# Cross attention in a decoder trunk: the queries of two heads as seven block products, laid between halves of keys and values

## The chip, the cores and the metric

The kernel runs on one core of one Trainium2 chip. The metric is the device time of one execution in microseconds (us). All data are float32; the matrix products are made by TensorE from two parts of each operand.

## The reference, cut to what matters

A trunk of two layers over 512 tokens of 1024 columns. Each layer runs a feed-forward network (FFN), a token mixer (layer 0: differential attention, layer 1: a pooling mixer), the cross attention into 256 memory tokens, and a second FFN, each followed by a layer norm. The change is in the cross attention:

```python
def memory_cross_attention(x, mem, wq, wkv, wo):      # x (1, 512, 1024), mem (1, 256, 1024)
    q = (x @ wq).reshape(B, S, 4, 256)                # 4 heads of 256 columns
    k, v = jnp.split(mem @ wkv, 2, axis=-1)
    ...
    s = jnp.einsum('bshd,bmhd->bhsm', q, k) * 256 ** -0.5
    p = jax.nn.softmax(s, axis=-1)
    o = jnp.einsum('bhsm,bmhd->bshd', p, v).reshape(B, S, 1024)
    return o @ wo
...
x = layer_norm(a * x + memory_cross_attention(x, mem, ...), ln_g[i, 2], ln_b[i, 2])
```

## The kernel before

**Numbers in two parts.** An operand is split into a rounded high part (a copy on ScalarE, names ending in h: `wh`, `xh`) and a low part (a subtraction on VectorE, `wl`, `xl`); `split` does this (lines 120 and 121), `split_scaled` with a factor (124 to 126). A product is three matmuls, high x high, high x low, low x high: `mm3`, lines 205 to 207. So nearly all matmuls of the profile stand on these three lines, and are told apart by their tiles.

**Tokens and weights.** The tokens lie as X0 to X3 (128 tokens each). After a layer norm a token tile is transposed on TensorE (line 489, tile `pt`) and split into `xh` and `xl`, one tile for each half of the columns. Raw weights are fetched by SyncE's queue (`raw_cols`, line 233: 8 x 128 rows by 256 columns, 1 MB, tiles of 8 KB a partition) into two buffers `raw`, then split into `wh` and `wl` (five buffers of each in the stages outside the FFN).

**The cross attention.** Queries of a head are two column tiles of 128, each 8 k x 3 matmuls over 512 tokens into the tiles `xq`, then scaled and split into `q`. Keys of a head (`xa_k`) are two tiles of 8 x 3 matmuls over 256 memory tokens into `pk`; values (`xa_v`) two of 8 x 3 into `pv`. A head's attention (`xa_head`) makes scores `xs`, the softmax into `p`, transposes `pt`, and `xo`, split into `oT`. `xa_main` walks the four heads: keys and values, then queries. `weave` runs `xa_main` and lets `xa_side` (the heads' attention) advance one step each time the main work's estimated nanoseconds have grown by a gap of 2500; a head's side work starts 3000 after its queries are ready. The output projection (`to_tokens`, tiles `ps`) runs in two halves of four k, the second with the residual sum and the layer norm.

In layer 0 the memory is fetched (`load_memory`, line 1314, tiles `p`) while the attention before is still at its output projection, and transposed (line 1327) into `mem0` to `mem7`. In layer 1 the memory, the keys and values of heads 0 and 1 and the keys of head 2 are made between the pooling mixer's work (`early_kv`). There, a list `late` holds work of the last token tile, which `turn_late` runs between matmuls, so the first head's queries are made in two halves of 256 tokens. Two of the first weights of a stage are held back by `split_weights` until a given point of the layer norm (`GATES`).

**The FFN's form of a product.** The FFN already makes some products of two blocks by two blocks with seven products instead of eight (`second_factors` and `up`): with the tokens as halves of tokens by halves of columns, six further factors are formed from sums, of which tiles `xe` hold the split parts; the weights' sums are made by DMAs that add to what is in the tile (`accum_op`, issued on GpSimd's queue, line 666), between two uses of the same tile.

Of the kernel before, what the change touches and what calls it, by code (L numbers as in the profile page):

```python
# [17 lines left out]
P = 128  # L18
# [26 lines left out]
GATES = {"xa": (1, 2)}  # L45

# [63 lines left out]
class Trunk:  # L110
    def __init__(self, tc, a, out, upto=8):
        self.tc, self.nc, self.a, self.out, self.upto = tc, tc.nc, a, out, upto
        self.side, self.late, self.gates = [], [], []
        self.ln_next_gb, self.kv_bufs = None, 8
# [95 lines left out]
    def weave(self, main, side, gap, lead=0):  # L210
# [3 lines left out]
        for ns in main:  # L214
            self.clock += ns
# [44 lines left out]

    def raw_heads(self, w, c0):
# [30 lines left out]
    def rows(self, w, k0, kn, c0, homes=None):  # L292


        got = []
        for k in range(0, kn, 4):
            n = min(4, kn - k)
            raw = self.raw_tile((4, S))
            r0 = (k0 + k) * P
            self.nc.sync.dma_start(  # L300
                raw[:, :n], w[r0 : r0 + n * P, c0 : c0 + S].rearrange("(k p) n -> p k n", p=P)
            )
            if homes:
                got += [home() for home in homes]
                for j, t in enumerate(got):
# [151 lines left out]
    def turn(self, t, half, tag="px"):  # L457
# [6 lines left out]
        if self.ln_next == "ffn":  # L464
# [544 lines left out]
    def da_values(self, h, vs):  # L1009

        raw = self.raw_cols(self.a["da_w_qkv"][0], 2 * D + h * P)
        ws = self.wide(raw)
# [232 lines left out]
    def pool_mixer(self, layer, ln):  # L1245
# [37 lines left out]
        wg = self.wide(self.pool_w)  # L1283
        self.begin_ln(layer, ln, 1.0)
        for t in range(NT):
# [16 lines left out]
            self.turn_late()  # L1302
# [33 lines left out]
    def xa_kv(self, w, h):  # L1336
        kt = self.keys.pop(0) if self.keys else (yield from self.xa_k(w, h))
        return kt, (yield from self.xa_v(w, h))

    def xa_k(self, w, h, raw=None, then=None, turn=True):  # L1340
        rk = raw or self.raw_cols(w, h * 256)
        ps = self.mm("pk").rearrange("p (c n) -> p c n", c=2)
        for j in range(2):
            with self.after(self.x_split if raw and not then else ()):
                wk = self.cols(rk, j)
            if then and j == 1:
                then()
            for k in range(KC):
                yield self.mm3(
                    ps[:, j], (wk[0][:, k], wk[1][:, k]), self.memT[k], k == 0, k == KC - 1  # L1350
                )
        kt = self.kv_tiles((P, 2, MEM))
        if turn:
            self.turn_late()
# [8 lines left out]
    def xa_v(self, w, h, raw=None):  # L1363
        wv = self.wide(raw or self.raw_cols(w, D + h * 256))
# [10 lines left out]
    def xa_head(self, qs, kt, v):  # L1375
# [34 lines left out]
        for c in range(2):  # L1410
# [4 lines left out]
            o = self.pair("oT")  # L1415
            self.split(o[0], o[1], po)
            self.oT.append(o)
            yield

    def early_kv(self, layer, ln, heads, raws):  # L1420
        w, keys = self.a["xa_wkv"][layer], {}

        def load_more():
            keys[1] = self.raw_cols(w, 256)
# [7 lines left out]
        self.keys.append((yield from self.xa_k(w, heads, turn=False)))  # L1432
# [191 lines left out]
```

## Time and profile before

| | us |
|---|---|
| runs | 1934.05, 1938.31, 1939.21 (median 1938.31) |
| profiled execution | 1932.35 |
| its span in the trace | 1930.6 |
| PE busy | 1902.1 (99%) |
| DVE, ACT, POOL busy | 1566.3, 1022.2, 315.0 (81%, 53%, 16%) |
| mean granted clock of TensorE | 0.998 |

In the rows of the profile, PE is TensorE's matmuls, PEld its weight loads, DVE is VectorE, ACT ScalarE, POOL GpSimd and SP SyncE; "q" behind a name is the engine's queue. A row of a timeline gives the start, the time, the engine, the line, the operation, out<-in, the shape and, in brackets, the idle time ahead of it with what ended it. A matmul's duration overlaps the next one's: the interval between two starts is what it costs in a stream. A row of a window gives the stretch, its length, busy time and count of PE, PEld, DVE, ACT and POOL, the granted clock, the share of the DMA engines and GB/s. A row of DMA issues ends with KB each and the median us from issue to landing.

### The profile page before, as it was taken

To read this page: it belongs to the slowest core of one execution; us is meant where nothing else is said; L and a number is where in the kernel's file an instruction comes from. 1 tells how busy PE (TensorE), PEld (TensorE's weight loads), DVE (VectorE), ACT (ScalarE), POOL (GpSimd) and SP (SyncE) were. 2 spreads that over 40 slices of the span, in tenths; PEclk is the share of its full clock that TensorE was granted. 3 is DMA by queue.
4 is the path that set the end of the run, shared out by engine and by line. 5 is a ranking of instruction groups with operands and counts; after the bars stand their busy time and mean duration, and the time that the engine had idled before them with its cause. 6 is when DMAs were issued, how large, how long until landed. Compare 5 with 4: busy or idle time off the path is not lost.

```text
span 1930.6 us, 32520 instructions
## 1 busy us (share of the span) xinstructions
PE 1902.1 (99%) x13114; PEld 1740.5 (90%) x13114; DVE 1566.3 (81%) x2200; ACT 1022.2 (53%) x1580; POOL 315.0 (16%) x276
## 2 busy tenths in 40 slices
PE   8999999999999999999999999999999999999998
PEld 8999998888778888999998999999889889999997
DVE  7888889888867557888888988898887568988886
ACT  6555454567655435655554655455445436555553
POOL 2112121111210001211210321112040012111210
PEclk9999999999999999999999999999999999999999
DMA  9978772322134316977686587778244356867861
GB/s 239 220 169 182 175 138 77 90 80 74 48 117 142 110 66 186 186 175 164 139 194 179 104 179 168 177 162 185 89 153 134 115 140 120 181 158 170 183 133 56
DMA packets 246743, 277.96 MB, mean 144 GB/s; under 512 B 8256, under 2 KB 212544, under 8 KB 246592
## 3 DMA queue, kind: packets, MB, share of 16 engines
q0 software_dynamic: 92928, 92.29, 31.1%
q1 hardware_dynamic: 153664, 183.59, 29.2%
q8 instruction: 103, 1.69, 0.3%
q14 instruction: 48, 0.39, 0.1%
HBM read 273.75 MB, written 2.10 MB: 143 GB/s over the span
## 4 chain that ended last, share of the span: by engine, by line
PE 80%; DVE 12%; ACT 3%; DMA 2%; issue 2%; POOL 1%; SPq 1%; DVEq 0%; ACTq 0%; POOLq 0%
PE x L205 7%; PE x L206 7%; PE x L207 7%; PE z L206 4%; PE z L205 4%; PE z L207 4%; PE ps L205 4%; PE ps L207 4%; PE ps L206 4%; PE px L205 2%; PE px L207 2%; PE px L206 2%; DVE wl L121 2%; PE y L207 2%; PE x L681 2%
## 5 line engine op out<-in xcount | busy, mean ns | idle before, releaser
L666 POOL DMA_DIRECT2D ra<-in_ffn_w_in_dram x132 | 170.3, 1309 | 993.5 <-DVE wl L121 815.2
L120 ACT CAST wh<-ra 128x1024 fp32r<-128x1024 f32 x184 | 193.7, 1053 | 218.9 <-PE x L206 67.5
L121 DVE TENSOR_TENSOR wl<-ra,wh 128x1024 fp32r<-128x1024 f32 x184 | 223.8, 1220 | 73.0 <-ACT wh L120 72.5
L120 ACT CAST wh<-rc 128x1024 fp32r<-128x1024 f32 x136 | 143.1, 1053 | 118.6 <-PE x L206 43.1
L205 PE MATMUL x<-xe,wh 128*128 128x256 f32 x704 | 195.0, 277 | 0.0
L206 PE MATMUL x<-xe,wh 128*128 128x256 f32 x704 | 194.8, 277 | 0.0
L207 PE MATMUL x<-xe,wl 128*128 128x256 f32 x704 | 194.8, 277 | 0.0
L121 DVE TENSOR_TENSOR wl<-rc,wh 128x1024 fp32r<-128x1024 f32 x136 | 164.6, 1219 | 28.4 <-ACT wh L120 28.1
L120 ACT CAST wh<-b 128x1024 fp32r<-128x1024 f32 x112 | 117.8, 1052 | 131.3 <-PE x L206 67.7
L121 DVE TENSOR_TENSOR wl<-b,wh 128x1024 fp32r<-128x1024 f32 x112 | 136.7, 1220 | 40.2 <-ACT wh L120 40.2
L205 PE MATMUL x<-xh,wh 128*128 128x256 f32 x544 | 151.1, 278 | 0.0
L206 PE MATMUL x<-xl,wh 128*128 128x256 f32 x544 | 150.6, 277 | 0.0
L207 PE MATMUL x<-xh,wl 128*128 128x256 f32 x544 | 150.6, 277 | 0.0
L206 PEld LDWEIGHTS x<-xe,wh 128*128 128x128 f32 x704 | 132.5, 188 | 1.4
L205 PEld LDWEIGHTS x<-xe,wh 128*128 128x128 f32 x704 | 132.1, 188 | 1.3
L207 PEld LDWEIGHTS x<-xe,wl 128*128 128x128 f32 x704 | 132.2, 188 | 0.0
L121 DVE TENSOR_TENSOR wl<-raw,wh 128x1024 fp32r<-128x1024 f32 x64 | 81.8, 1285 | 38.8 <-ACT wh L120 38.2
L206 PEld LDWEIGHTS x<-xl,wh 128*128 128x128 f32 x544 | 102.5, 188 | 0.7
L205 PEld LDWEIGHTS x<-xh,wh 128*128 128x128 f32 x544 | 102.1, 188 | 0.7
L207 PEld LDWEIGHTS x<-xh,wl 128*128 128x128 f32 x544 | 102.1, 188 | 0.0
L207 PE MATMUL y<-xh,wl 128*128 128x256 f32 x352 | 98.4, 280 | 1.2
L206 PE MATMUL z<-xl,wh 128*128 128x256 f32 x352 | 97.5, 277 | 0.7 <-DVE xl L121 0.7
(429 smaller groups left out, 6291.6 us busy)
## 6 DMA issues: line engine op xcount, KB each, us to landing
ra<-in_ffn_w_in_dram POOLq DMA_DIRECT2D x132, 512.0 KB, 6.7
rc<-in_ffn_w_in_dram SPq DMA_DIRECT2D x88, 512.0 KB, 5.8
b<-in_ffn_w_out_dram SPq DMA_DIRECT2D x76, 512.0 KB, 4.8
ra<-in_ffn_w_in_dram SPq DMA_DIRECT2D x44, 512.0 KB, 5.4
rc<-in_ffn_w_in_dram POOLq DMA_DIRECT2D x44, 512.0 KB, 6.7
raw<-in_xa_wkv_dram SPq DMA_DIRECT2D x16, 1024.0 KB, 5.4
raw<-in_da_w_qkv_dram SPq DMA_DIRECT2D x16, 512.0 KB, 5.2
raw<-in_xa_wq_dram SPq DMA_DIRECT2D x8, 1024.0 KB, 4.9
```

Of the source, the lines that this page charges most:

```text
L120: self.nc.scalar.copy(hi, src),
L121: self.nc.vector.tensor_sub(lo, src, hi.bitcast(F32)),
L205: mm(out, w[0], x[0], start=start, stop=False, skip_group_check=again)
L206: mm(out, w[0], x[1], start=False, stop=False, skip_group_check=again)
L207: self.last_mm = mm(out, w[1], x[0], start=False, stop=stop, skip_group_check=again)
L666: nc.gpsimd.dma_start(t, source(*block), accum_op=ALU.add)
L681: self.last_mm = nc.tensor.matmul(ps[:, j], v[i][:, k, j * P : (j + 1) * P], x[l][:, k], start=n == i == l == 0, stop=n == 7 and i == 1, s ...
```

## The change

For each layer, the queries of heads 0 and 1, and of heads 2 and 3, are now one product of two blocks by two blocks each (`xa_queries`: 512 tokens as two halves, 1024 columns as two halves of k, two heads as two column blocks), made by seven products of 24 matmuls over 256 tokens. Factors 0 and 1 are the tokens 0 and 1 as they were; the other factors come from `xa_factors`, which transposes tokens 2 and 3, forms the sums and splits them, in four steps. The weights' sums come from accumulating DMAs on GpSimd's queue. `XA_ORDER` lays the parts out by hand for each layer: a digit is the next part (half of keys, half of values) of that head, "q" and "r" the next product of the first and second pair, "s" the next step of the factors, "Q" and "R" the point from which a pair's two heads are open to the side work; a head's attention so can start only when its whole pair is done.

Around it, raw weights lie in tiles of 4 KB (half of a head's keys or values, 512 KB, or two k of the output's weights), five of them in layer 0, four in layer 1; the stage's `wh` and `wl` have four buffers, not five; `pT`, `oT` and `q` have fewer or wider buffers, and later `oT` tiles and the layer norm's gains use the six factor tiles `xe`. The weave's gap is 2100. The diff, without small helpers:

```diff
+XA_ORDER = ("0000s00ss" "qq1q11qq1q11qQ" "r222r2r22rr3rrR33333", "qsqs2qsq2sq3qqQ" "r2r3rr33rrrR33")
...
+    def raw_quarter(self, w, r0, c0, width):
+        raw = self.raw_tile((4 * 256 // width, width))
+        rows = w[r0 : r0 + P * 4 * 256 // width, c0 : c0 + width]
+        self.last_load = self.nc.sync.dma_start(raw, rows.rearrange("(k p) n -> p k n", p=P))
+        return raw
+    def raw_keys(self, w, h):
+        return [self.raw_quarter(w, 0, h * 256 + j * P, P) for j in range(2)]
+    def raw_values(self, w, h):
+        return [self.raw_quarter(w, r, D + h * 256, 256) for r in (0, S)]
...
-        for j in range(0, 8, 4):
+        for half in raw:
             t = self.hl([P, 4, 256])
-            self.split_weights(t[0], t[1], raw[:, j : j + 4])
+            self.split_weights(t[0], t[1], half)
...
+        got, n = [], self.raw_rows
+        for k in range(0, kn, n):
+            raw = self.raw_tile((n, S))
             r0 = (k0 + k) * P
...
-        if self.ln_next == "ffn":
+        if self.ln_next != "da":
...
-    def xa_kv(self, w, h):
-        kt = self.keys.pop(0) if self.keys else (yield from self.xa_k(w, h))
-        return kt, (yield from self.xa_v(w, h))
-
-    def xa_k(self, w, h, raw=None, then=None, turn=True):
-        rk = raw or self.raw_cols(w, h * 256)
+    def xa_kv(self, w, h, turn=None):
+        kt = self.keys.pop(0) if self.keys else None
+        if not kt:
+            kt = yield from self.xa_k(w, h, turn=turn)
+            yield None
+        self.kv.append((kt, (yield from self.xa_v(w, h))))
+    def xa_k(self, w, h, raw=None, then=None, turn=None):
+        rk = raw or self.raw_keys(w, h)
         ps = self.mm("pk").rearrange("p (c n) -> p c n", c=2)
         for j in range(2):
+            wk = self.hl([P, KC, P])
             with self.after(self.x_split if raw and not then else ()):
-                wk = self.cols(rk, j)
+                self.split_weights(wk[0], wk[1], rk[j])
             if then and j == 1:
                 then()
             for k in range(KC):
                 yield self.mm3(
                     ps[:, j], (wk[0][:, k], wk[1][:, k]), self.memT[k], k == 0, k == KC - 1
                 )
+            yield None
...
-            o = self.pair("oT")
-            self.split(o[0], o[1], po)
-            self.oT.append(o)
+            if c == 0:
+                o = self.pair("oT" if len(self.oT) < 4 else "xe", (P, 2, S))
+            self.split(o[0][:, c], o[1][:, c], po)
+            self.oT.append((o[0][:, c], o[1][:, c]))
...
+    def xa_factors(self):
+        nc, F, H = self.nc, self.factors, 2 * P
+        a11, a12, a21, s1 = (self.tmp("oT", (P, 4, H)) for i in range(4))
+        def part(i, x, o=slice(0, H)):
+            self.split(F[i][0][:, :, o], F[i][1][:, :, o], x)
+        for t in (2, 3):
+            o = slice(t % 2 * P, (t % 2 + 1) * P)
+            pts = []
+            for half in range(2):
+                pt = self.aux("pt", ("py", "yz")[half]).rearrange("p (c n) -> p c n", c=4)
+                c0 = half * S
+                with self.behind():
+                    self.transpose4(pt, [self.X[t][:, c0 + j * P : c0 + (j + 1) * P] for j in range(4)])
+                pts.append(pt)
+            nc.scalar.copy(a21[:, :, o], pts[0])
+            nc.vector.tensor_tensor(s1[:, :, o], pts[1], a21[:, :, o], ALU.subtract)
+            part(3, s1[:, :, o], o)
+            part(2, pts[1], o)
+            yield
+        for r, (hi, lo) in zip((a11, a12), F):
+            nc.vector.tensor_tensor(r, hi.bitcast(F32), lo.bitcast(F32), ALU.add)
+        s2, s4, s3 = s1, a12, a21
+        nc.vector.scalar_tensor_tensor(s2, s1, -1.0, a11, ALU.mult, ALU.subtract)
+        nc.vector.scalar_tensor_tensor(s4, s2, -1.0, a12, ALU.mult, ALU.subtract)
+        part(6, s4)
+        yield
+        part(4, s2)
+        nc.vector.tensor_tensor(s3, a11, a21, ALU.subtract)
+        part(5, s3)
+        yield
+    def xa_queries(self, w, h, q):
+        nc, H = self.nc, 2 * P
+        def source(row, col):
+            c0 = (h + col - 1) * H
+            return w[(row - 1) * S : row * S, c0 : c0 + H].rearrange("(k p) n -> p k n", p=P)
+        def load(*block):
+            t = self.raw_tile((4, H))
+            nc.sync.dma_start(t, source(*block))
+            return t
+        def more(t, *block):
+            nc.gpsimd.dma_start(t, source(*block), accum_op=ALU.add)
+        def operand(raw):
+            v = self.hl([P, 4, H])
+            self.split_weights(v[0], v[1], raw)
+            return v
+        def product(ps, v, a, start=False):
+            x = self.factors[a]
+            for j in range(2):
+                o = slice(j * P, (j + 1) * P)
+                for k in range(4):
+                    yield self.mm3(
+                        ps[:, j], (v[0][:, k, o], v[1][:, k, o]), (x[0][:, k], x[1][:, k]),
+                        start and j == k == 0, j == 1 and k == 3, True,
+                    )
+        bank = lambda t: t.rearrange("p (j n) -> p j n", j=2)
+        halves = slice(0, H), slice(H, S)
+        scale = (D // XA_H) ** -0.5
+        def done(i, half, src, by):
+            hi, lo = (t[:, :, halves[half]] for t in q[i])
+            self.split_scaled(hi, lo, src, by)
+        ra = load(1, 1)
+        x = bank(self.aux("x", "px"))
+        v = operand(ra)
+        more(ra, 1, 2)
+        rc = load(2, 1)
+        yield from product(x, v, 0, True)
+        p1 = self.tmp("p", (P, 2, H))
+        nc.scalar.copy(p1, x)
+        yield None
+        y = bank(self.aux("y", "yz"))
+        v = operand(rc)
+        rd = load(2, 2)
+        yield from product(y, v, 1, True)
+        nc.vector.tensor_tensor(p1, y, p1, ALU.add)
+        q[0] = self.pair("q", (P, 2, S))
+        done(0, 0, p1, scale)
+        yield None
+        z = bank(self.aux("z", "yz"))
+        v = operand(ra)
+        more(ra, 2, 2)
+        yield from product(z, v, 3, True)
+        p5 = self.tmp("p", (P, 2, H))
+        nc.scalar.copy(p5, z)
+        yield None
+        v = operand(rd)
+        more(rd, 1, 2)
+        yield from product(z, v, 6)
+        yield None
+        v = operand(ra)
+        more(ra, 2, 1)
+        yield from product(x, v, 4)
+        u2 = self.tmp("p", (P, 2, H))
+        q[1] = self.pair("q", (P, 2, S))
+        nc.scalar.copy(u2, x)
+        nc.vector.tensor_tensor(u2, z, u2, ALU.add)
+        done(1, 0, u2, -scale)
+        yield None
+        yield from product(x, operand(rd), 5)
+        nc.vector.tensor_tensor(p5, x, p5, ALU.add)
+        done(1, 1, p5, -scale)
+        yield None
+        yield from product(x, operand(ra), 2)
+        done(0, 1, x, scale)
+        yield None
+    def part(self, units):
+        for ns in units:
+            if ns is None:
+                return
+            yield ns
     def xa_main(self, layer):
         wq, wkv = self.a["xa_wq"][layer], self.a["xa_wkv"][layer]
-        early = len(self.kv)
-        for h in range(XA_H):
-            if h >= len(self.kv):
-                self.kv.append((yield from self.xa_kv(wkv, h)))
-            kt, v = self.kv[h]
-            raw = self.raw_cols(wq, h * 256)
-            qs = []
-            ws = [self.cols(raw, c) for c in range(2)]
-            ps = [self.mm("xq") for c in range(2)]
-            for p in ((0, 2 * P), (2 * P, S)) if self.late else ((0, S),):
-                for c in range(2):
-                    yield from self.project(ps[c], ws[c], (p,))
-                    self.turn_late(max(len(self.late) - 1, 0) if c == 0 else 0)
-            for c in range(2):
-                q = self.pair("q")
-                self.split_scaled(q[0], q[1], ps[c], (D // XA_H) ** -0.5)
-                qs.append(q)
-            self.heads.append((self.clock, (qs, kt, v)))
-            if 0 < early and h + early < XA_H:
-                self.kv.append((yield from self.xa_kv(wkv, h + early)))
+        self.late, second = [], self.xa_factors()
+        qs = [[None] * 2 for n in range(2)]
+        works = {n: self.xa_queries(wq, 2 * i, qs[i]) for i, n in enumerate("qr")}
+        works.update((str(h), self.xa_kv(wkv, h)) for h in range(1, XA_H))
+        works["0"] = self.xa_kv(wkv, 0, lambda: next(second))
+        for n in XA_ORDER[layer]:
+            if n == "s":
+                next(second)
+            elif n in "QR":
+                i = "QR".index(n)
+                for j in range(2):
+                    q = [(qs[i][j][0][:, c], qs[i][j][1][:, c]) for c in range(2)]
+                    self.heads.append((self.clock, 2 * i + j, q))
+            else:
+                yield from self.part(works[n])
...
-            while h >= len(self.heads) or self.clock < self.heads[h][0] + 3000:
+            while h >= min(len(self.heads), len(self.kv)) or self.clock < self.heads[h][0] + 3000:
                 yield WAIT
-            yield from self.xa_head(*self.heads[h][1])
...
-        bufs = dict(q=8, oT=10, gb=2)
+        bufs = dict(xe=6, q=4, oT=4)
+        self.raw_rows = 2
         if layer == 0:
             self.kv, self.keys = [], []
             mem = self.side_pool("mem")
-            with self.other_pools():
+            with self.stage_pools(4, dict(raw=5), ("wh", "wl", "raw")):
                 self.stage["mem"] = mem
-                with self.phase_pool(("gb", "gb"), "p", pT=6, p=4, kv=8, _x=0, **bufs):
+                with self.phase_pool(("xe", "xe"), "p", pT=4, p=4, kv=8, _x=0, **bufs):
                     self.kvp = self.phase["kv"]
                     with self.tc.high_priority():
                         self.load_memory("p")
                     self.xa(layer, ln)
             self.close_side()
         else:
-            with self.later, self.phase_pool(("gb", "gb"), "p", _x=0, pT=6, p=4, **bufs):
+            with self.later, self.phase_pool(("xe", "xe"), "p", _x=0, pT=4, p=4, **bufs):
                 self.xa(layer, ln)
     def xa(self, layer, ln):
-        self.heads, self.oT = [], []
-        self.weave(self.xa_main(layer), self.xa_side(), 2500)
+        self.heads, self.oT, self.factors = [], [], self.factor_tiles()
+        self.weave(self.xa_main(layer), self.xa_side(), 2100)
         self.begin_ln(layer, ln, 1.0)
         kv = lambda: self.kv_tiles((P, S))
-        homes = [[lambda: self.pair("q")] * 4, [kv] * 4]
+        wide = [self.pair("q", (P, 2, S)) for k in range(2)]
+        views = [tuple(t[:, i] for t in pair) for pair in wide for i in range(2)]
+        homes = [[lambda v=v: v for v in views], [kv] * 4]
...
-            self.later.enter_context(self.other_pools(("wh", "wl", "mem", "raw")))
+            self.later.enter_context(self.stage_pools(4, dict(raw=4), ("wh", "wl", "mem", "raw")))
...
-                raws = [self.raw_cols(w, c) for c in (0, D)]
+                raws = [self.raw_keys(w, 0), self.raw_values(w, 0)]
...
```

More of the change, by code (lines that the diff above doesn't have):

```diff
@@ L214, in weave @@
         for ns in main:
+            ns = ns or 0
             self.clock += ns
@@ L1431, in early_kv @@
             self.kv.append((kt, (yield from self.xa_v(w, h, raws[1] if h == 0 else None))))
-        self.keys.append((yield from self.xa_k(w, heads, turn=False)))
+        self.keys.append((yield from self.xa_k(w, heads)))
+    def xa_factors(self):
[28 more added lines that the diff above has]
+        yield
```

27 lines of the change are left out of this document (13 added, 14 removed).

## The prediction, before the result

> **What bounds the kernel now.** I read the page first: busy shares, granted clock, chain.
>
> ```profile
> span 1930.6 us, 32520 instructions
> PE 1902.1 (99%) x13114; PEld 1740.5 (90%) x13114; DVE 1566.3 (81%) x2200; ACT 1022.2 (53%) x1580; POOL 315.0 (16%) x276
> PEclk9999999999999999999999999999999999999999
> PE 80%; DVE 12%; ACT 3%; DMA 2%; issue 2%; POOL 1%; SPq 1%; DVEq 0%; ACTq 0%; POOLq 0%
> ```
>
> TensorE is busy 99% of the span at a granted clock that never leaves the top tenth, and it carries 80% of the chain that ended last. Then I asked for the windows of the changed stage: layer 0's first head, the rest of its heads, and the heads of layer 1.
>
> ```profile
> 605.00:630.00 25.00, 25.00 (x172) 22.82 (x171) 14.88 (x21) 11.14 (x20) 0.00 (x0) 1.00 0.54 168
> 630.00:702.00 72.00, 72.00 (x447) 63.68 (x445) 38.40 (x60) 31.58 (x61) 0.00 (x0) 1.00 0.36 118
> 1492.00:1544.00 52.00, 52.00 (x306) 45.26 (x305) 27.32 (x47) 22.23 (x47) 0.00 (x0) 1.00 0.31 106
> ```
>
> In all three PE (first figure after the length) has no idle time, and VectorE (third pair) has 40 to 47% to spare. Two things follow. Every matmul taken out here shortens the run by its full time, and every new wait of PE costs its full time, since nothing of before's waits is there to be paid with it.
>
> **What is removed.** The price of a matmul is the interval between starts, since the durations overlap.
>
> ```profile
> L205 PE MATMUL xq<-xh,wh 128*128 128x512 f32 x112 | 45.1, 403 | 0.0
> L205 PE MATMUL x<-xe,wh 128*128 128x256 f32 x704 | 195.0, 277 | 0.0
> 605.04 0.40 PE L205 MATMUL xq<-xh,wh 128*128 128x512 f32 x1
> 616.24 0.28 PE L205 MATMUL pk<-mem0h,wh 128*128 128x256 f32 x1
> 618.97 0.28 PE L205 MATMUL pk<-mem0h,wh 128*128 128x256 f32 x1
> ```
>
> From 605.04 to 616.24 stand the 48 matmuls of head 0's queries (two column tiles, eight k, three products): 11.20 us, 0.2333 each. From 616.24 to 618.97 stand 24 of half the columns: 2.73 us, 0.1138 each. Before, the queries take 7 heads x 48 = 336 at 512 columns (112 on each of three lines, as the first row counts) and 96 at 256 for the eighth head, whose tokens are taken by halves: 336 x 0.2333 + 96 x 0.1138 = 78.4 + 10.9 = 89.3 us. After: seven products x 24 x four pairs of heads = 672 at 256 columns, 76.5 us. **Gain 12.8 us**; all other matmuls are the same in number. If the new ones run at 0.118 the gain is 10.0; if the eighth head's 96, which transposes interrupt, were worth 0.12, 13.4.
>
> **What is added beside PE.** Per layer VectorE gets six factors' sums and low parts and some more low halves of weights; by the count of instructions about 22 us more a layer, and ScalarE about 14. The same kinds of operation stand in the FFN's entry, back to back:
>
> ```profile
> 1605.20 1.28 DVE L380 SCALAR_TENSOR_TENSOR X<-X,rstd,gb 128x1024 f32<-128x1024 f32 x1
> 1606.40 0.68 DVE L631 TENSOR_TENSOR hb<-pt,hb 128x512 f32<-128x512 f32 x1
> 1607.00 1.21 DVE L611 TENSOR_TENSOR hb<-xh,xl 128x1024 f32<-128x1024 f32 x1
> 1608.14 0.68 DVE L121 TENSOR_TENSOR xl<-hb,xh 128x512 fp32r<-128x512 f32 x1
> ...
> 1622.01 1.22 DVE L121 TENSOR_TENSOR xe<-sr,xe 128x1024 fp32r<-128x1024 f32 x1
> 1623.14 1.22 DVE L644 TENSOR_TENSOR hb<-hb 128x1024 f32<-128x1024 f32 x1
> ```
>
> By intervals a scaled sum of 1024 columns costs 1.20 us, a plain one or a low half 1.13 to 1.14, one of 512 0.60. Over the whole stage the addition is hidden: 605 to 702 has 53.3 us of VectorE in 97, so about 75 in 90 afterwards. What matters is where it is needed at once. There are three such places.
>
> **Place 1: entry of layer 0.** The built program shows something the diff only implies. With the raw tiles at 4 KB and the extra factor tiles, the memory's raw tiles (p) now lie over tiles of the attention before: the first of the four loads waits for the last ps<-low matmuls and stands in SP's queue behind weight loads, the others wait for ScalarE's square of token 3 (rt). Before, they were issued 30 us earlier.
>
> ```profile
> 559.25 2.69 SPq L1314 DMA_DIRECT2D p<-in_mem_dram  x4
> 588.73 0.39 PE L207 MATMUL ps<-p,oT 128*128 128x512 f32 x1
> 590.64 0.88 PE L1327 MATMUL pt<-ident,p 128*128 128x128 f32 x6 [0.16 <-DVE xl L121]
> 591.27 0.36 PE L205 MATMUL pk<-mem0h,wh 128*128 128x256 f32 x1
> 590.51 0.67 DVE L357 SCALAR_TENSOR_TENSOR X<-X,ps 128x512 f32<-128x512 f32 x1
> 593.40 1.15 ACT L374 ACTIVATE rt<-X,mean 128x1024 bf16<-128x1024 f32 x1 [0.99 <-DVE mean L366]
> p<-in_mem_dram SPq DMA_DIRECT2D x4, 256.0 KB, 3.1
> ```
>
> Before, keys start at 591.27. After, token 3's sum ends about 590.5 on VectorE (no memory low halves stand ahead of it), one weight low half (1.13) and the mean follow, the square runs from about 591.9 to 593.1. Four issues took 2.69 us before; the first is released earlier here, so I put the last at about 594.0. It lands 3.1 later at 597.1, and its transposes (six took 0.88, four about 0.6) and their cast bring the keys to about 597.9. PE has nothing to fill this: in its order the 16 transposes and the 48 matmuls of keys stand right behind the last ps. **Loss 6.6 us**, 5 if the square comes a microsecond sooner and loads overlap better, 8 if the loads share the engines with the weight loads ahead of them.
>
> **Place 2: first pair of layer 0.** The weights' sums are made by accumulating DMAs on POOL's queue. After the third product (z) has split its weights, its tile takes one more block for the fifth product. Between the two PE has the 24 matmuls of z and about 12 others (2 of keys, 8 of scores, 2 of the fourth product): 36 x 0.114 = 4.1 us. The rest of the keys and the fourth product, which could hide the wait, stand behind the fifth product's first matmuls on PE.
>
> ```profile
> ra<-in_ffn_w_in_dram POOLq DMA_DIRECT2D x132, 512.0 KB, 6.7
> ra<-in_ffn_w_in_dram POOLq DMA_DIRECT2D x3, 512.0 KB, 5.9
> ra<-in_ffn_w_in_dram POOLq DMA_DIRECT2D x3, 512.0 KB, 9.6
> L120 ACT CAST wh<-ra 128x1024 fp32r<-128x1024 f32 x184 | 193.7, 1053 | 218.9 <-PE x L206 67.5
> ```
>
> The first row is the median of the run, the others are those of 764 to 782 us (quiet SP queue) and of 735 to 760 (DMA share 0.81). The stage has a share of 0.54, nearer to the quiet case: 6.2 + 1.05 for the cast = 7.3 against 4.1. **Loss 3.2 us** (2.5 to 4.5 from 5.9 and the median, more in a rival). The Trainium skill, "DMA: Bandwidth & Descriptors", section "Anatomy of one DMA — SWDGE (gpsimd) path", fits such a transfer by 2.0 us plus its bytes at 436 GB/s: for 512 KB an estimate of 3.2 us, and the sum would be 3.2 us lower. The trace's 5.9 to 9.6 us for an accumulating one disagree, and the measurement decides.
>
> **Place 3: first pair of layer 1.** Here no keys or values of head 0 are left to cover the factors. VectorE's order from token 3's mean to the low part of the factor that the fourth product needs holds 7 weight low halves (7.9 us), 4 plain sums or low parts of 1024 (4.6), 4 scaled ones (4.8) and 9 of 512 columns (5.4): 22.7 us.
>
> ```profile
> 1461.74 1.28 DVE L380 SCALAR_TENSOR_TENSOR X<-X,rstd,gb 128x1024 f32<-128x1024 f32 x1 [0.32 <-POOL rstd L376]
> 1462.95 1.22 DVE L247 TENSOR_TENSOR wl<-raw,wh 128x1024 fp32r<-128x1024 f32 x1
> 1467.90 1.06 PE L489 MATMUL pt<-ident,X 128*128 128x128 f32 x8 [0.47 <-DVE X L380]
> 1464.55 0.28 PE L205 MATMUL xq<-xh,wh 128*128 128x256 f32 x1
> ```
>
> Before, the instruction at this point starts at 1462.95; after, one more weight low half (1.13) stands ahead of it and I allow 0.4 for the mixer's fourth weight buffer, so about 1464.5, and the factor is ready at 1487.2. PE meanwhile has from 1464.55 (delayed by about 1) three products, head 2's values and 2 of keys, 122 x 0.1138 = 13.9 us, and 16 transposes (2 x 1.06): done at 1481.6. **Stall 5.6 us**, 4 to 7. Before's 0.47 there is not saved, it becomes part of it.
>
> **The rest.** The last xo stands inside the next projection's group: about +0.5 us. The second pairs have 9 us or more of PE work between each accumulating load and its use, so nothing (up to 2). Plain loads halve in size and double in number on SP's queue; the DMA share of 0.36 to 0.54 hides them. The pooling mixer has four weight buffers instead of five: nothing, +-1.
>
> **Sum** on the profiled execution: 1932.35 (span 1930.6) - 12.8 + 6.6 + 3.2 + 5.6 + 0.5 = 1935.45, **+3.1 us**. The median of the runs is 1938.31, so 1941.4. With all ends together: -13.4 + 5 + 2.5 + 4 + 0 - 1 = -2.9 to -10 + 8 + 4.5 + 7 + 0.5 + 3 = +13; as these don't all fall one way, 1935 to 1949 for this case.
>
> **Rivals.**
> A. *The gain comes through.* Places 1 and 3 cost little: the memory loads go out as the attention's tiles come free, earlier than I chained them, and the factors of layer 1 keep ahead of PE. For it: VectorE's spare share of the windows, and the same construction in the FFN's entry, where VectorE runs the whole chain between 1605 and 1623. Against it: the waits stand in the program, and PE's order has nothing to slide in. With 1 us left at each: -12.8 + 1 + 1 + 3.2 + 0.5 = about -7, so 1931. Chance 0.24.
> B. *Accumulating loads are slow in the whole stage* (slower). They share the engines with SP's weight loads, as in the 9.6 us row. Then place 2 costs 9.6 + 1.05 - 4.1 = 6.6, and in the second pairs, where 9 us of cover stand against 10.7, three steps a layer lose 1.7: 10 us in all. Sum 3.1 + 3.4 + 10 = +16.5, so 1955; it decides from about 8 us a load on. Half of that is likelier: 1949. Chance 0.17.
> C. *Halving the columns does not halve a matmul* (slower). Each one carries a weight load of 188 ns, and if that set the pace at 256 columns, 672 x 0.188 = 126 us would replace 89, +37 us. Against it: 0.1138 us between starts in row upon row. Chance 0.04. The Trainium skill, "TensorE: Matmul & The Clock Gate", section "Back-to-back issue gap", gives a sustained spacing of about 81 ns at 128 columns and 131 at 512; between them an estimate of 98 at 256 makes the queries 53 us before and 66 after, so a loss of 13 in place of the gain. The trace shows 113.8 and 233.3, in proportion, and decides.
>
> **How the numbers follow.** The forecast's case has 0.55. A measurement of this kernel tells about 0.3%, 5.8 us, from no change: of that case 0.35 lies within it, 0.19 above +5.8, 0.01 below -5.8. Faster: 0.25. Same: 0.35. Slower: 0.19 + 0.17 + 0.04 = 0.40. The range takes in A's value and the lower half of B: 1929 to 1951.
>
> **What would show it.** In the profile after: 672 matmuls at 256 columns about 0.114 apart and no xq at 512; the memory loads issued after 590 with PE idle about 6 us before the first pk of layer 0; an idle time of about 3 us ahead of the fifth product's x<-xe near 620, ended by the cast of an accumulated tile; and one of about 5 us near 1482, ended by VectorE's low part of xe. It is wrong if PE stays busy through these three places, or if idle time shows ahead of the second pairs or in the mixer of layer 1.

## The result: slower by 1%, and the profile after

| | before | after |
|---|---|---|
| median of the runs, us | 1936.37 (4 runs) | 1955.26 (4 runs, 1953.64 to 1957.92) |
| profiled execution / span, us | 1932.35 / 1930.6 | 1954.08 / 1952.1 |
| ratio to before, 95% interval | | 1.0099 [1.0085, 1.0113] |

The forecast was 1941.4 in 1929 to 1951; the measured time is 18.9 us over before's and outside the range. The page of the changed kernel, first the rows that answer to those of before:

```profile
span 1952.1 us, 33221 instructions
PE 1903.1 (97%) x13354; PEld 1754.3 (90%) x13354; DVE 1606.5 (82%) x2244; ACT 1048.0 (54%) x1614; POOL 336.8 (17%) x292
PEclk9999999999998999999999999999999999999999
PE 73%; DVE 15%; DMA 4%; ACT 4%; issue 2%; POOL 1%; SPq 1%; DVEq 0%; ACTq 0%; POOLq 0%
```

Two differences of these rows hold the whole loss. The span less PE's busy time, its idle time, went from 1930.6 - 1902.1 = 28.5 to 49.0 us: 20.5 us more. And PE's busy time rose by 1.0 us where 12.8 less were counted. VectorE got 40 us and ScalarE 26 more, where 44 and 28 were counted. In the chain PE lost 7 points of its share; DVE and DMA took five of them, ACT one.

PE's longest waits (what waited, for what, us in total, times, longest), before and after; the waits for X's load are the kernel's start:

```profile
PE pt L489 <- DMA X<-in_x_dram: 7.1, 2, 4.1
PE ps L206 <- DVE wl L121: 3.1, 1, 3.1
PE sc L1070 <- DVE a L121: 1.7, 2, 1.3
```

```profile
PE pt L1345 <- DMA p<-in_mem_dram: 9.2, 3, 7.7
PE pt L506 <- DMA X<-in_x_dram: 6.4, 2, 4.2
PE pt L506 <- DVE xl L124: 3.8, 1, 3.8
PE ps L209 <- DVE wl L124: 2.9, 1, 2.9
PE x L208 <- ACT wh L123: 2.5, 1, 2.5
```

The three foreseen places are there, with their times in the timelines:

```profile
592.18 2.22 SPq L1332 DMA_DIRECT2D p<-in_mem_dram  x4
...
596.04 0.66 PE L1345 MATMUL pt<-ident,p 128*128 128x128 f32 x2 [7.68 <-DMA p<-in_mem_dram]
...
601.37 0.56 PE L208 MATMUL pk<-mem0h,wh 128*128 128x256 f32 x1
...
630.97 0.58 PE L208 MATMUL x<-xe,wh 128*128 128x256 f32 x1 [2.53 <-ACT wh L123]
...
1487.01 1.04 ACT L123 CAST wh<-raw 128x1024 fp32r<-128x1024 f32 x1 [4.18 <-DMA raw<-in_xa_wkv_dram]
...
1490.66 1.08 PE L506 MATMUL pt<-ident,X 128*128 128x128 f32 x4 [3.82 <-DVE xl L124]
...
1498.46 2.20 ACT L123 CAST wh<-raw 128x1024 fp32r<-128x1024 f32 x2 [3.88 <-DMA raw<-in_xa_wq_dram]
...
1500.71 0.38 PE L208 MATMUL pk<-mem0h,wh 128*128 128x256 f32 x1 [0.95 <-ACT wh L123]
...
1502.14 0.38 PE L208 MATMUL z<-xe,wh 128*128 128x256 f32 x1 [0.93 <-ACT xe L123]
```

```profile
p<-in_mem_dram SPq DMA_DIRECT2D x4, 256.0 KB, 5.1
```

The memory's loads go out at 592.18, as worked out, PE idles 7.7 us for the first of them, they take 5.1 us to land in the median, and the keys start at 601.37. The fifth product's first matmul waits 2.5 us for the cast of an accumulated tile. In layer 1 PE waits 3.8 us, not for the factors' sums but for token 3's low half, whose VectorE queue stood behind a weight cast on ScalarE that a late load held up for 4.2 us. Waits near the factors come later, four between 1500 and 1504 (0.95, 0.93, 0.56 and 0.31 us); the first is for weights that ScalarE cast only after waiting 3.9 us for an accumulating load.

What the prediction had no term for is in the windows (length, busy time and count of PE, PEld, DVE, ACT, POOL, then the granted clock):

```profile
586.00:604.00 18.00, 8.80 (x43) 7.28 (x42) 13.17 (x18) 7.57 (x13) 2.49 (x2) 0.72 0.59 175
592.83:603.07 10.24, 5.52 (x24) 4.75 (x25) 6.34 (x8) 2.80 (x7) 1.08 (x1) 0.50 0.87 256
...
630.38:637.19 6.81, 6.22 (x29) 6.22 (x30) 2.36 (x2) 1.92 (x3) 2.43 (x2) 0.50 0.98 216
632.00:638.00 6.00, 6.00 (x33) 6.00 (x33) 1.48 (x3) 1.24 (x2) 1.29 (x1) 0.57 1.06 198
...
638.00:704.00 66.00, 63.26 (x520) 61.51 (x519) 41.93 (x62) 34.30 (x61) 5.12 (x4) 1.00 0.61 150
...
1490.54:1493.93 3.39, 3.27 (x16) 3.30 (x17) 3.39 (x5) 1.88 (x3) 1.32 (x1) 0.50 0.50 149
1504.19:1507.59 3.40, 3.40 (x18) 3.40 (x17) 1.80 (x2) 1.82 (x2) 0.11 (x1) 0.50 1.13 170
```

With each of these groups of waits the granted clock falls. From 632 to 638 PE is busy all the time and gets 33 matmuls done, where 6 us hold 52 at 0.1138. The starts there stand 0.21 us apart:

```profile
632.21 0.41 PE L208 MATMUL pk<-mem0h,wh 128*128 128x256 f32 x1
632.42 0.41 PE L209 MATMUL pk<-mem0l,wh 128*128 128x256 f32 x1
```

So a wait of 2.5 us is followed by 6.2 us at half pace (630.97 to 637.2): 29 matmuls, which at 0.1138 take 3.3 us, so 2.9 are lost. In the four stretches that the clock spends at 0.50, PE works 5.52 + 6.22 + 3.27 + 3.40 = 18.4 us; in the same proportion about 8.6 us of that are lost, well over half of the 13.8 by which PE's busy time is over the count. (A fifth stretch, in the mixer, has its like in the trace of before.) Another 1.7 us lie in the matmuls: the 672 new ones take 82.1 us from start to start, or to their own end where PE then waits, of which 2.2 are the half clock's, and before's 432 took 91.0 by the same measure. That is a gain of 11.1 and not 12.8. The other 3.5 I could not place.

### The profile page after: what moved, and what is told of

Same layout as the page of the kernel before. It is cut to its first block, busy times and chain, and to the rows that moved or that the text cites. A ratio compares the mean times of both kernels' runs of the same rounds, so it can differ in the third digit from the quotient of the medians.

```text
span 1952.1 us, 33221 instructions
## 1 busy us (share of the span) xinstructions
PE 1903.1 (97%) x13354; PEld 1754.3 (90%) x13354; DVE 1606.5 (82%) x2244; ACT 1048.0 (54%) x1614; POOL 336.8 (17%) x292
## 4 chain that ended last, share of the span: by engine, by line
PE 73%; DVE 15%; DMA 4%; ACT 4%; issue 2%; POOL 1%; SPq 1%; DVEq 0%; ACTq 0%; POOLq 0%
PE x L208 7%; PE x L209 7%; PE x L210 7%; PE z L210 4%; PE z L209 4%; PE z L208 4%; PE ps L210 4%; PE ps L208 4%; PE ps L209 4%; DVE wl L124 3%; PE px L208 2%; PE px L210 2%; PE px L209 2%; DMA ra<-in_ffn_w_in_dram 2%; PE y L210 2%
## 5 line engine op out<-in xcount | busy, mean ns | idle before, releaser
L208 PE MATMUL x<-xe,wh 128*128 128x256 f32 x768 | 213.4, 278 | 3.2 <-ACT wh L123 2.5
L209 PE MATMUL x<-xe,wh 128*128 128x256 f32 x768 | 212.7, 277 | 0.0
L210 PE MATMUL x<-xe,wl 128*128 128x256 f32 x768 | 212.5, 277 | 0.0
L208 PE MATMUL x<-xh,wh 128*128 128x256 f32 x608 | 169.1, 278 | 0.3 <-DVE p L1574 0.3
L210 PE MATMUL x<-xh,wl 128*128 128x256 f32 x608 | 168.4, 277 | 0.6 <-DVE wl L251 0.6
L209 PE MATMUL x<-xl,wh 128*128 128x256 f32 x608 | 168.4, 277 | 0.0
L208 PEld LDWEIGHTS x<-xe,wh 128*128 128x128 f32 x768 | 144.3, 188 | 5.2 <-ACT wh L123 2.7
L209 PEld LDWEIGHTS x<-xe,wh 128*128 128x128 f32 x768 | 144.7, 188 | 1.4
L210 PEld LDWEIGHTS x<-xe,wl 128*128 128x128 f32 x768 | 144.2, 188 | 0.0
L124 DVE TENSOR_TENSOR wl<-raw,wh 128x1024 fp32r<-128x1024 f32 x76 | 96.1, 1269 | 37.0 <-ACT wh L123 36.4
L208 PEld LDWEIGHTS x<-xh,wh 128*128 128x128 f32 x608 | 114.2, 188 | 1.3 <-DVE p L1574 0.5
L123 ACT CAST wh<-raw 128x1024 fp32r<-128x1024 f32 x76 | 79.2, 1049 | 59.7 <-DMA raw<-in_xa_wq_dram 15.2
```

What stands on the lines that cost most here:

```text
L123: self.nc.scalar.copy(hi, src),
L124: self.nc.vector.tensor_sub(lo, src, hi.bitcast(F32)),
L208: mm(out, w[0], x[0], start=start, stop=False, skip_group_check=again)
L209: mm(out, w[0], x[1], start=False, stop=False, skip_group_check=again)
L210: self.last_mm = mm(out, w[1], x[0], start=False, stop=stop, skip_group_check=again)
```

## The experiments

After the result I held two theories. **A**: the loss is the idle time in these places, each lengthened by its half-clock stretch; take a place away and its time comes back. **B**: the stage is late for another reason, and the time comes back elsewhere. Each median stands beside before's from the same chip. Longer edits are given in words within their diffs. Runs 5, 6 and 10 to 12 leave out part of the computation, so they tell of time alone.

**1. The memory early.** One line: the keys' buffers come first, so the memory's raw tiles lie over tiles that are free 30 us sooner.

```diff
-with self.phase_pool(("xe", "xe"), "p", pT=4, p=4, kv=8, _x=0, **bufs):
+with self.phase_pool(("xe", "xe"), "p", kv=8, p=4, pT=4, _x=0, **bufs):
```

> The changed kernel with one edit: in layer 0's cross attention the keys' and values' buffers are laid first and the memory's raw tiles behind them, so that these lie over tiles that the attention before leaves early; its loads go out about 30 us sooner, as before the change. Theory A (the loss is idle time of PE in a few places, each lengthened by a stretch at half the granted clock): the entry wait of 7.9 + 1.3 us goes and the half clock from 594 to 603 us with it, 10 us in all; in the built order z6 now stands ahead of the fifth product, which gives place 2 about 4 us more cover, so its 2.7 us and the 6 us at half clock behind it go too (about 5.5): 1955 - 15 = about 1940 us. Rival B (the stage is slower whatever starts it: more work on VectorE, more and smaller loads): the time comes back in the stage and at most 4 us are gained, 1951.

Measured 1954.32 beside 1933.99, ratio 1.0101 [1.0086, 1.0116]: nothing gained, and theory A falls in this form. The entry's wait is gone (the keys start at 591.6 in place of 601.4), yet new ones stand behind it. From the timeline of this kernel, in the order of the argument:

```profile
612.27 0.58 PE L210 MATMUL y<-xh,wl 128*128 128x256 f32 x1 [3.44 <-DVE wl L124]
...
639.52 0.58 PE L208 MATMUL x<-xe,wh 128*128 128x256 f32 x1 [5.74 <-ACT p L1569]
...
637.94 1.04 ACT L123 CAST wh<-raw 128x1024 fp32r<-128x1024 f32 x1 [7.61 <-DMA raw<-in_xa_wq_dram]
...
638.89 0.58 ACT L1569 COPY p<-x 128x512 f32<-128x512 f32 x1
...
628.67 1.29 POOL L1511 DMA_DIRECT2D raw<-in_xa_wq_dram  x1 [5.50 <-DVE wl L124]
```

The second product waits for its low half, since VectorE has factor sums queued ahead of it. The fifth step's product waits for the copy of line 1569, which frees its bank; that copy stands on ScalarE behind the cast of the last block's weights, and the cast waits for an accumulating load issued at 628.67, 9.3 us earlier. Arriving earlier only made PE wait longer for the same chain of loads, casts and sums.

**2. The fourth block fetched later**, so that head 2's values find a free raw tile in layer 1.

```diff
         v = operand(rc)
-        rd = load(2, 2)
 ...
         more(ra, 2, 2)
+        rd = load(2, 2)
```

> The changed kernel with one line moved: the fourth block of weights (rd) is fetched behind the third product's accumulating load instead of ahead of the second product, so that in layer 1 the second half of head 2's values finds a free raw tile at once. Theory A: the 4.0 us wait of PE near 1486 us, which I put down to that load (ScalarE and VectorE stand behind the split of the late weights), and the half clock behind it (about 2 us) go; the factors' chain on VectorE stays and takes about 2 us of it back: 1951. Rival: the wait is VectorE's amount of work, not the load; then the wait moves to the fourth product and the time stays, 1955.

1956.03 beside 1933.99, 1.0111 [1.0096, 1.0127]: no gain. The load came in time, but the accumulating load of the first tile took its place at the head of ScalarE's queue:

```profile
1485.92 1.04 ACT L123 CAST wh<-raw 128x1024 fp32r<-128x1024 f32 x1 [4.51 <-DMA raw<-in_xa_wq_dram]
```

It was issued at 1477.74, 8.2 us before. VectorE stood still for 4.7 us there. So neither the named load alone nor VectorE's amount of work made this wait, but a queue with two late loads in it.

**3. Eight products in place of seven**: no sums, no accumulating loads, 96 matmuls more.

```diff
-        more(ra, 1, 2) ... seven products with factors 0, 1, 3, 6, 4, 5, 2 and sums of products
+        x: blocks (1,1) and (2,1) by factors 0, 1;  y: the same blocks by tokens 2, 3
+        x: blocks (1,2) and (2,2) by factors 0, 1;  y: the same blocks by tokens 2, 3
 in xa_factors:
-        the sums s1 to s4 and factors 4 to 6
+        part(3, pts[0], o); part(2, pts[1], o)
```

> The changed kernel with eight block products in place of seven: same tiles, same order of parts, but no sums of tokens, no accumulating loads, and 24 matmuls of 256 columns more for each pair (96 in all, 10.9 us of PE at 0.1138). Theory A: the entry of layer 0 stays as it is (10 us); the wait and half clock of place 2 (5.5 us) and those of the factors in layer 1 (about 3.5 us idle, 2 to 3 at half clock) go, and some of the second pairs' (3 us): 1955 + 10.9 - 13 = about 1953. If the sums cost PE nothing, the time is 10.9 more, 1966. If the seven products themselves run slower than counted, it is well below 1950.

1947.18 beside 1933.99, 1.0063 [1.0048, 1.0078]. With 10.9 us of PE's work added it is faster than the changed kernel by 0.36%, about 7 us. With the entry still late, what feeds the seven products costs some 18 us, more than they save. Theory A's 1953 was too high. The other cause that was named, seven products that run slower than counted, is priced by run 10 below, at 2.7 us.

**4. PE kept busy through the entry's wait** by 64 transposes that nobody reads.

```diff
+            idle = self.aux("idle", "yz")
+            with self.behind():
+                for i in range(64):
+                    self.nc.tensor.transpose(idle[:, :P], self.ident, self.ident)
```

> The changed kernel with 64 transposes of the identity into an unused tile between the last matmul of the attention before and the memory's transposes in layer 0, about 7 us of PE's 8 us of idle time there; nothing reads their output. The memory's loads are as late as before. Theory A with the clock as a term of its own: the granted clock stays at 1.00 through 586 to 604 us, the memory's 16 transposes and the first keys run at full pace, and the run is 2 to 3 us shorter: 1952.5. Rival (the half clock is only how an idle PE is shown, and the transposes wait for the loads anyway): 1955, or a little more.

1957.97 beside 1933.99, 1.0120 [1.0103, 1.0137]. The clock stayed up, as the window shows against 0.72 in the changed kernel, and the run got no shorter:

```profile
586.00:604.00 18.00, 15.34 (x118) 13.77 (x117) 14.48 (x20) 8.63 (x15) 2.49 (x2) 1.00 0.56 176
...
642.23 1.04 ACT L123 CAST wh<-raw 128x1024 fp32r<-128x1024 f32 x1 [4.62 <-DMA raw<-in_xa_wq_dram]
```

As in experiment 1, the pair's chain of casts and loads comes next: here too a cast stands first on ScalarE and holds it for 4.6 us at 642. Since this edit moved that order as well, the price of the half clock by itself stays open.

Theory A in its new form, **A2**, was that the chain's accumulating loads are the larger part of the loss; its rival, called C in what follows (not the prediction's rival C), that VectorE's sums are.

**5 and 6. Accumulating loads out; factor sums out** (the entry still late).

```diff
5:  -            nc.gpsimd.dma_start(t, source(*block), accum_op=ALU.add)
    +            nc.sync.dma_start(t, source(*block))
6:  -        a11, a12, s2, s4, s3 and part(6), part(4), part(5)
    +        (left out; the products take factors 2 and 3 for 6, 4 and 5)
```

> The changed kernel with the 16 accumulating loads replaced by plain loads of the same blocks on SP's queue (the tile is overwritten, so the weights' sums are left out and the queries are others). Everything else stays, the factors' sums too. Theory A2 (what costs is the time of accumulating loads, 6 to 9 us from issue to landing, in the fixed order of the engines: in the run with the memory early, ScalarE's cast of the last block waited 7.6 us for one that landed 9.2 us after its issue, with the copy that PE's next product needs queued behind it): a plain load lands in 3.5 to 5 us, the wait of place 2 and part of those of layer 1 and the second pairs go, 1955 - 8 to 10 = about 1946. Rival C (the sums on VectorE hold PE up): little changes, 1952 to 1955.

> The changed kernel without the sums and splits of factors 4 to 6 (VectorE: two plain sums, two scaled ones, one difference and three low parts of 1024 columns, about 9.3 us a layer; ScalarE three casts); the three products take factors 2 and 3 in their place, so the queries are others. Accumulating loads stay. Theory A2: layer 0 changes little, in layer 1 the 1.1 + 1.1 + 0.8 + 0.6 us of waits for the factors and the half clock behind them go, about -4: 1951. Rival C: the whole loss beyond the entry goes, -10 or more, 1945.

1945.35 and 1949.14 beside 1935.48: 1.0052 [1.0037, 1.0067] and 1.0068 [1.0053, 1.0083]. Either one helps by 0.3 to 0.5%; the loads as theory A2 had it, the sums by 0.3% where A2 gave 0.2 and rival C 0.5 or more. Edit 5 changes two things at once, the adding and the queue that issues the load (GpSimd's, then SyncE's); no run parts them, and "accumulating loads" stands for both in what follows.

**7. The copy put ahead of the cast**, on top of experiment 1.

```diff
+        with self.tc.issue_after(copy.ins):
+            nc.scalar.copy(v[0], ra)
+        with self.tc.issue_after(add.ins):
+            nc.vector.tensor_sub(v[1], ra, v[0].bitcast(F32))
```

> The kernel of the run with the memory early, and one order fixed: ScalarE's cast and VectorE's low part of the last block's weights stand behind the copy and the sum that free the product's bank for the fifth product, instead of ahead of them. Theory A2: the 5.9 us wait of PE at 633 us goes but for a microsecond or two, and the half clock behind it (639 to 644 us at 0.19 instead of 0.114 us a matmul, about 2); the same in the other pairs where the cast stood first: 1954 - 7 = about 1947. Rival C: the order does not matter, since VectorE is late by itself: 1953.

1953.18 beside 1935.48, 1.0089 [1.0072, 1.0106]. The copy now goes out at once and PE's 5.7 us for it are gone; but the cast still waits for its load, 6.1 us, and behind it PE has a new wait of 2.0 us (the row of line 1574). Of the 7 us expected 0.1% is seen at most. Part of what layer 0 won was lost in layer 1, where PE's wait for token 3 grew from 2.9 to 4.3 us:

```profile
PE pt L506 <- DVE xl L124: 4.3, 1, 4.3
PE y L210 <- DVE wl L124: 4.2, 5, 3.6
...
PE x L208 <- DVE p L1574: 2.3, 2, 2.0
```

**8. Eight products and the memory early** (edits 1 and 3).

> Eight block products (no sums, no accumulating loads) and the memory's loads early as in the first experiment. PE's work then stands 1.9 us below that before the change (96 matmuls back of the 12.8 us). Theory A2: without the pair's chain nothing takes the place of the entry's wait, so its 10 us come off this time: from 1.0063 to about 1.001 of the time before, 1936 to 1938 beside 1934. Rival B (the entry's wait covers work that would be late anyway): 1.005 or more.

1936.48 beside 1935.48, 1.0005 [0.9996, 1.0015]. Here the edit that brought nothing in experiment 1 brings its whole 0.58%, 11 us: with no chain behind the entry, PE goes through layer 0's attention with hardly any idle time. The run also clears what came along with the change (smaller raw tiles, four weight buffers, the gap of 2100): with all of that in place, the memory early and as many columns through PE as before, the time is that of before within 0.15%.

```profile
592.00:756.00 164.00, 163.91 (x1174) 153.17 (x1173) 99.08 (x156) 68.95 (x129) 8.06 (x7) 1.00 0.40 116
```

**10, 11 and 12. The square with the memory early**: neither accumulating loads nor sums (10), sums alone (11), accumulating loads alone (12). Edits as in 5 and 6.

> Seven products with everything taken out that feeds them in a chain: memory early, plain loads in place of the accumulating ones, no sums for factors 4 to 6 (the three products take factors 2 and 3), so the queries are others. Theory A2 (the gain of 12.8 us is there, and the chain of loads and sums eats it): PE has the work of the changed kernel without its waits; what stays are the mixer's 1.4 us and some waits of layer 1's entry, 3 to 4 us: 1935.5 - 12.8 + 4 = about 1927, 0.995 to 0.996. Rival (the products themselves cost more than counted): 0.999 or more.

> Memory early and plain loads in place of the accumulating ones, the sums of factors stay (the queries are others). With the run with the memory early (both stay, 1.0101) and the one with neither (0.9962) this and the next run make a square. Theory A2 (the accumulating loads, by the order of the engines behind them, are the larger part): the 3.6 us for the second product's low half at 608 may stay, since VectorE's sums stand ahead of it, the 5.9 us at 633 goes, layer 1 keeps some 5 us for its factors: about 1.001. Rival C (VectorE's sums): 1.006 or more.

> Memory early and no sums and splits of factors 4 to 6 (the three products take factors 2 and 3, the queries are others), the accumulating loads stay. Theory A2: the wait behind ScalarE's cast at 633 us and the one of 4 to 5 us near 1481 us in layer 1 stay, the one at 608 goes: about 1.004. Rival C (VectorE's sums are the larger part): 0.999 or less.

| memory early, ratio to before | plain loads | accumulating loads |
|---|---|---|
| no sums | 0.9962 [0.9946, 0.9977] (10) | 1.0035 [1.0023, 1.0047] (12) |
| sums | 1.0028 [1.0016, 1.0039] (11) | 1.0101 [1.0086, 1.0116] (1) |

Accumulating loads cost 0.0073, sums 0.0066, both together 0.0139, as much as the two added: about 14 and 13 us. Run 11 came out between what A2 and C gave, run 12 near A2's 1.004; the two costs differ by less than the intervals, so neither is shown to be "the larger part". The waits fit. In 11 the second product's wait of experiment 1 is still there and the copy's is gone; in 12 it is the other way round:

```profile
PE y L210 <- DVE wl L124: 3.6, 1, 3.6
```

```profile
PE x L208 <- ACT p L1560: 4.2, 2, 2.8
PE pt L506 <- DVE xl L124: 3.6, 1, 3.6
```

Run 10 shows the products themselves: its 672 matmuls take 79.2 us by the measure above, against 76.5 counted and 91.0 for the queries of before, and the kernel is faster than before by 0.38%, where 0.4 to 0.5% was expected.

**9. The version that the runs point to**: memory early, the first pair of each layer by eight products, the second by seven, with the sums between the pairs.

```diff
-XA_ORDER = ("0000s00ss" "qq1q11qq1q11qQ" "r222r2r22rr3rrR33333", "qsqs2qsq2sq3qqQ" "r2r3rr33rrrR33")
+XA_ORDER = ("0000s00" "qq1q11qq1q11qQ" "ssr222r2r22rr3rrR33333", "qsqs2qq2q3qqQ" "ssr2r3rr33rrrR33")
 in xa_queries: the first pair as in experiment 3, the second as in the change
 in xa_factors: tokens 2 and 3 split as they are first, the difference for factor 3 later
```

> A version that the runs point to: memory early; the first pair of each layer by eight block products (no sums and no accumulating loads while VectorE is busy with the layer norm), the second pair by seven, with the factors' sums made in between. Against the run with eight products in both pairs (1.0005 of the time before), PE has 48 matmuls less, 5.5 us. Theory A2: in the second pairs the accumulating loads have 9 us or more of PE work between issue and use, and the waits there were 3.2 us in layer 0 and 0.5 in layer 1 in the changed kernel, so 2 to 4 us of the 5.5 remain: 0.998 to 0.999, about 1933 beside 1935.5. Rival C (the sums alone fill VectorE): 1.001 to 1.003.

1932.48 (11 runs) beside 1935.09, 0.9988 [0.9979, 0.9997]: as expected, and the only version here with all of the computation that lies below both kernels; against before by 0.12%, with the interval's end just under 1.

## Why the prediction was wrong, by its own steps

- **What bounds the kernel** held: PE was the bound before. **What is removed** held but for a microsecond: the new matmuls stand 0.114 us apart at the median, and by run 10 (91.0 - 79.2) 11.8 of the 12.8 us are there.
- **Place 1** had the right mechanism and issue time (592.2) but was too small, 10.1 us instead of 6.6. The last load landed at 599.6, not at 597.1: the four took 5.1 us in the median where 3.1 were counted, with a weight load issued just ahead of them and two behind. And the transposes and first keys ran at 0.5 to 0.73 of the clock. The 8 us of the upper end weren't enough.
- **Place 2** was right in its wait (2.5 to 2.7 us, forecast 3.2) and lacked the stretch at half clock behind it, 2.9 us. (The side remark there is off a little: with 3.2 us for the load the term would be 0.15, so the sum 3.05 lower, not 3.2.)
- **Place 3** failed in its cause. VectorE's 22.7 us of work were counted as running without a gap; in fact VectorE itself stood still for 3.9 us, behind ScalarE's cast of a late load. Then came the four waits of 1500 to 1504, 2.75 us. Forecast 5.6, measured 6.6 us of idle time and the half clock.
- **The second pairs** were put at nothing (up to 2) and had 2.7 us of waits in layer 0, all in the heads' attention that runs between them (`xo` for `pT`, `pt` for `p`), none for a product's load. **The mixer** was put at nothing and got a new wait of 1.4 us.
- **The sum** is the step that failed most, in two ways. It had no term for the clock. In the profiled executions its waits come to 15.9 us against 20.5 us of added idle time; the half clock took about 8.6 more, where nothing was put; and PE's other work fell by some 7.6 us in place of 12.8. And it added places as if each were a cost of its own. Experiments 1 and 8 show that they are not: the same edit is worth 0 or 11 us, depending on whether the chain behind it is there. The changed stage was no longer bound by PE with gaps, but by the chain that feeds the products.
- **Rival B** (accumulating loads slow in the whole stage) gave 1949 to 1955, with a chance of 0.17. That its 1955 is the measured time is luck: 11 of the 16 loads took 5.8 to 6.0 us, the other five 6.7 to 8.5, and the 10 us that it put into the second pairs weren't lost there. What it had right is the feeder: with the memory early, the accumulating loads are half of what the chain costs. **Rival A** did not hold: the FFN's entry runs the same construction with waits of PE of at most 0.7 us, and why this stage doesn't was not tested. **The prediction's rival C**, a wider spacing of the narrow matmuls, is refuted by the 0.114 us at 256 columns.
- What the text named as a sign that it is wrong came true in part: idle time in the mixer and beside the second pairs, though not at their products.

## What to carry to other kernels

Price a trade of matmuls for sums and loads by the chain that feeds the matmuls, not by the matmuls alone and not by the waits one by one: take out each feeder alone, and both, and see whether they add. When a cure for the longest wait brings nothing, look at the next wait on the same chain before doubting the cure, and try it again once that chain is short. A step that waits for a load delays whatever its engine has queued behind it, as ScalarE's cast did here for 7.6 us; the longer and less even the load, the further ahead it should be issued.

## What the runs showed of the hardware

One long wait is not what loses the granted clock of TensorE. In the changed kernel it fell at 630.4, in a wait of 2.5 us, and at 1504.2, after four waits of 0.95 us and less; single waits of 1.2 us (689.9) and 1.4 us (1449.3) did not lose it. The 3.4 us ahead of the two falls, and a stretch as long with the 1.4 us in it, behind which the clock stayed at 1.00:

```profile
626.96:630.37 3.41, 1.29 (x8) 1.05 (x8) 2.75 (x3) 0.63 (x2) 0.13 (x1) 1.00 0.93 156
1500.78:1504.18 3.40, 1.60 (x7) 1.00 (x8) 3.40 (x4) 2.25 (x3) 1.39 (x2) 1.00 0.80 104
...
1446.16:1449.57 3.41, 1.98 (x16) 1.69 (x15) 3.41 (x4) 2.51 (x5) 3.41 (x3) 1.00 0.00 0
```

PE was busy for 1.29 and 1.60 us ahead of the falls, less than half, and for 1.98, more than half, where the clock stayed. So in these places the busy share of some 3.4 us goes with the fall, and not the length of a single wait; no run was made to find the limit. At half pace the clock stayed for 3.4 us (1490.5 and 1504.2), 6.8 (630.4) or 10.2 (592.8). The Trainium skill, "TensorE: Matmul & The Clock Gate", section "HAM oscillation — how this bites in real kernels", has the rule of no idle gaps over about 3.4 us; here gaps of 2.5 us and of under 1 us were enough, and the measurement decides.

Accumulating loads of 512 KB took 5.8 to 6.0 us in 11 of the changed kernel's 16, and 6.7 to 8.5 in five. Of the two longest, the one at 632.6 was issued 2.4 us behind another of its kind, and the one at 1478.7 had a load of SP's queue 0.9 us behind it; but the one at 650.2 took 6.0 beside two loads of SP's queue, so what makes one long is not shown. The median is the row

```profile
raw<-in_xa_wq_dram POOLq DMA_DIRECT2D x16, 512.0 KB, 6.0
```
